# Attention: the products of probabilities and values of two column blocks issued as one run

## Chip, cores and metric

One core of a Trainium2 chip runs the kernel. The metric is the device time of one execution in microseconds; the time of the kernel before is the median of three runs.

## What is computed

One layer of an encoder over 1024 tokens of 1024 channels, float32 throughout: a norm, a wide input projection, four branches (a gated linear recurrence, neighbourhood attention, a state space mixer, pooling), gates, and output products. Only the attention branch is changed. Cut to what matters (8 heads of 64 channels, 16 rows of 64 tokens, 4 column blocks of 16 columns; a block sees 32 columns of 8 rows):

```python
def one_row(r):
    rs = jnp.clip(r - kr // 2, 0, rows - kr)
    k_blk = lax.dynamic_slice_in_dim(kg, rs, kr, axis=1)[:, :, kcol]
    v_blk = lax.dynamic_slice_in_dim(vg, rs, kr, axis=1)[:, :, kcol]
    sc = jnp.einsum('bjqhd,brjkhd->bhjqrk', q_r, k_blk)
    sc = jnp.where(mask, sc + bias[None], -1e30)
    pr = jax.nn.softmax(sc.reshape(sc.shape[:4] + (kr * NA_BAND,)), axis=-1).reshape(sc.shape)
    return jnp.einsum('bhjqrk,brjkhd->bjqhd', pr, v_blk)
```

The changed lines are those of the last einsum, probabilities times values.

## The kernel before

Large products (`mm3`, lines 93 to 95) split each operand into a high and a low part and make three passes of a float32r matmul each. They make up most of the program: the input projection (`z_gen`, `tok_gen`), the merge and the output.

Attention runs in four rounds (`rd`), two heads each. `at_units` goes over two groups of eight rows (`g`) and four column blocks (`j`), so 32 blocks in all, each of 128 queries by 384 keys. A block does the following for its two heads `h`:

- six score matmuls into `ps_s` (line 514), head 0 on partitions 0 to 63 and head 1 on 64 to 127 of the operands;
- bias, maximum, exponential, sum and scaling on DVE and ACT, in the tile `sc` (four buffers);
- three transposes per head into `ps_t` (line 98), copied by ACT into `PT` (line 80; three buffers);
- six products of probabilities and values into `ps_o` (line 536): for each of three key chunks `c`, head 0 (64 columns of the array, output partitions 0 to 63) and then head 1 (output partitions 64 to 127). They are plain float32, and each shows in the trace as two matmuls with a weight load each, so 12 a block and 384 in all. Below, "value products" are these.

The four blocks of a group share one `ps_o` tile, a PSUM bank. When the group is done, ACT copies it into `yb`, and after two groups one DMA writes `yb` out (line 541).

Between two blocks the generator yields, and one piece of other work is emitted: in rounds 0 and 1 the projection for the round two ahead (`at_z`, 24 matmuls of 256 columns a piece, `ps_z`), afterwards pieces of the input projection for other branches (`fill`, 24 matmuls of 512 columns, `ps_z`). So TensorE has two sorts of work in this stage.

The emitted order is not the executed order. The program is built with `schedule_with_timeline_sim=True`: a planner orders the instructions of each engine when the program is built, by dependencies, free buffers and its own estimates of durations. Each engine then executes its queue strictly in that order and waits on semaphores. `add_manual_dep` with the class `NoSync` gives the planner an edge (this one after that one) and adds no semaphore.

The values of a round are in `vb` (one buffer), loaded by 16 DMAs on SP's queue at the start of the round (line 490), with the bias DMAs (line 503) behind them in the same queue. Eleven small loads of constants (`vr`, `gr`, lines 228 to 239) are issued by GpSimd near the start; TensorE transposes them once.

Of the kernel before, what the change touches and what calls it, by code (L numbers as in the profile page):

```python
# [9 lines left out]
F32 = mybir.dt.float32  # L10
# [19 lines left out]
class Kern:  # L30
# [47 lines left out]
    def copy_a(self, out, a, scale=None):  # L78
        if scale is None:
            self.nc.scalar.activation(out, a, AF.Copy)  # L80
        else:
            self.nc.scalar.activation(out, a, AF.Copy, scale=scale)
# [5 lines left out]
    def mm3(self, ps, pairs):  # L88
        """ps = sum over (aH, aL, bH, bL) of a^T b, in three passes each."""
        n = len(pairs)  # L90
        mm = self.nc.tensor.matmul
        for k, (aH, aL, bH, bL) in enumerate(pairs):
            mm(ps, aH, bH, start=(k == 0), stop=False)  # L93
            mm(ps, aH, bL, start=False, stop=False)  # L94
            mm(ps, aL, bH, start=False, stop=(k == n - 1))  # L95
# [4 lines left out]
    def cmul(self, pool, outr, outi, ar, ai, br, bi, shape, neg_im=False):  # L100
        """(outr, outi) = a * b, elementwise complex."""
        t = pool.tile(shape, F32, tag="cm_t", name="cm_t")
        self.mul(outr, ar, br)
        self.mul(t, ai, bi)
        self.sub(outr, outr, t)
        u = pool.tile(shape, F32, tag="cm_u", name="cm_u")
        self.mul(outi, ar, bi)
        self.mul(u, ai, br)
        self.add(outi, outi, u)

    def rsqrt(self, pool, x, n, tag):
        """x [P, n] -> 1/sqrt(x), to float32 accuracy."""
        P = x.shape[0]
        g = pool.tile([P, n], F32, tag=tag + "_g", name=tag + "_g")
        h = pool.tile([P, n], F32, tag=tag + "_h", name=tag + "_h")
        self.ts(h.bitcast(I32), x.bitcast(I32), 1, None, ALU.arith_shift_right)
        self.ts(g.bitcast(I32), h.bitcast(I32), -1, 0x5F3759DF, ALU.mult, ALU.add)
        for _ in range(3):
            self.mul(h, g, g)
            self.stt(h, h, -0.5, x, ALU.mult, ALU.mult)  # L120
            self.stt(g, h, 1.5, g, ALU.add, ALU.mult)
        return g

    def dexp(self, pool, out, x, n):
        """out = exp(x), x [128, n], to float32 accuracy (underflow ends at 1e-38)."""
        t = [pool.tile([128, n], F32, tag=f"de{i}", name=f"de{i}") for i in range(4)]
        xc, nf, r, q = t
        self.ts(xc, x, 88.0, -87.0, ALU.min, ALU.max)
        self.ts(nf, xc, 1.4426950408889634, MAGIC, ALU.mult, ALU.add)
        self.ts(nf, nf, MAGIC, None, ALU.subtract)  # L130
        self.stt(r, nf, -0.693359375, xc, ALU.mult, ALU.add)
        self.stt(r, nf, 2.12194440e-4, r, ALU.mult, ALU.add)
        self.ts(q, r, 1.0 / 5040, None, ALU.mult)
        for c in (1.0 / 720, 1.0 / 120, 1.0 / 24, 1.0 / 6, 0.5, 1.0):
            self.stt(q, q, c, r, ALU.add, ALU.mult)
        self.ts(nf.bitcast(I32), nf, 127.0, 8388608.0, ALU.add, ALU.mult)
        self.stt(out, q, 1.0, nf, ALU.add, ALU.mult)

# [18 lines left out]
    def z_gen(self, parts):  # L157
        """z^T channel tiles. parts: (first column, number of 256-column blocks, consume), with
        consume(ct, half, psum[128 ch, 512 tok]); the weights of a tile are made ready one tile ahead."""
        todo = [(c0 + 256 * b, 2 * b, s, f) for c0, n, f in parts for b in range(n) for s in range(2)]  # L160
        raw = None
        ready = []

        def prep(k):
            nonlocal raw
            c, ct, s, f = todo[k]
            if s == 0:
                raw = self.wload_in(c)
            H, L = self.whl([128, 8, 128])
            self.split(H, L, raw[:, :, s * 128:(s + 1) * 128])  # L170
            ready.append((H, L, ct + s, f))
        prep(0)
        for k in range(len(todo)):
            if k + 1 < len(todo):
                prep(k + 1)
            H, L, ct, f = ready.pop(0)
            for hf in range(2):
                ps = self.ps(self.zt[hf])
                t = slice(hf * 512, hf * 512 + 512)
                self.mm3(ps, [(H[:, k, :], L[:, k, :], self.hnH[k][:, t], self.hnL[k][:, t])  # L180
                              for k in range(8)])
                yield 5.2, 0.55 + (f(ct, hf, ps) or 0.0)
# [5 lines left out]
    def drive(self, main, filler, scale=1.0):  # L188
        """emit main, with pieces of filler wherever the tensor engine would run dry."""
# [10 lines left out]
    def w_tok_halves(self, raw):  # L200
        """a [128, 8, 256] block as rhs: list over k of (H, L) [128, 256]."""
        out = []
        for kh in range(2):
            H, L = self.whl([128, 4, 256])
            self.split(H, L, raw[:, 4 * kh:4 * kh + 4, :])
            out += [(H[:, k, :], L[:, k, :]) for k in range(4)]
        return out

    def tok_gen(self, aH, aL, raw, consume):
        """token-layout product: consume(t, psum[128 tok, 256])."""  # L210
# [40 lines left out]
    def lru_consts(self):  # L251
        """softplus(-lambda) for the LRU, all channel tiles and both directions."""
# [23 lines left out]
    def rel_bias(self):  # L276
        """E[v, q, h, dr, 32]: bias along the band of each kind of column block."""
# [4 lines left out]
        with self.tc.tile_pool(name="nb", bufs=1, reuse_waits="tile") as tmp:  # L282
# [3 lines left out]
            # (v, first q, count, dst column of q0, its step, src column of q0, its step)  # L286
# [157 lines left out]
    def at_z(self, rd, raw=None):  # L444
        """first gives the tiles, then emits the product piece by piece."""
# [12 lines left out]
    def at_prep(self, ap, rd, z):  # L458
# [7 lines left out]
        for sd in range(2):  # L466
# [3 lines left out]
            for hf in range(2):  # L470
                pt = self.ps("t")
                for t in range(4):
                    o = pt[:, t * 128:t * 128 + 128]
                    if sd == 0:   # queries in the order (col block, row, col)
# [8 lines left out]
    def at_units(self, ap, rd, qk, bias, vd):  # L483
# [9 lines left out]
        for g in range(2):  # L493
# [12 lines left out]
            po = self.ps("o")  # L506
            for j in range(4):
# [8 lines left out]
                for h in range(2):  # L516
# [13 lines left out]
                    T = ap.tile([128, 384], F32, tag="PT", name="PT", bufs=3)  # L530
                    self.copy_a(T, pt[:, :384])
                    PT.append(T)
                qc = slice(j * 128, j * 128 + 128)
                for c in range(3):
                    for h in range(2):
                        nc.tensor.matmul(po[hp[h], qc], vb[:, g + c, j, h * 64:h * 64 + 64],  # L536
                                         PT[h][:, c * 128:c * 128 + 128], start=(c == 0), stop=(c == 2))
# [6 lines left out]
    def branch_gate(self, n, c0):  # L544
        """silu of a branch's gate, into DRAM."""
# [164 lines left out]
    def s5_params(self, kp, sp):  # L710
# [29 lines left out]
        # angles into [-pi, pi]; then the cosine's  # L740
# [14 lines left out]
        # powers a^0 .. a^8  # L755
# [10 lines left out]
        # zero-order hold  # L766
# [15 lines left out]
        # Bbar [(d p), g, 32], upper 16 columns zero  # L782
# [10 lines left out]
        # power tables: Q's, slot u: a^u (f), a^(9-u) (b)  # L793
# [8 lines left out]
        # G's, slot t: a^(7-t) (f), a^t (b), times e^{-i 8 theta}  # L802
# [10 lines left out]
        # phasors e^{+-i 8 theta 2^m}  # L813
# [8 lines left out]
        # C^T [(d p), (g c)]  # L822
# [10 lines left out]
        # D on the diagonal of the (quadrant, c) layout of K  # L833
# [13 lines left out]
    def s5_u(self):  # L847
        """c_x, permuted to [ch, t, j] (token 8j + t), into DRAM."""
# [22 lines left out]
    def s5_batch(self, sb, ct):  # L871
# [3 lines left out]
        def bcg(tab, n):   # [128, n, 32] -> [128, 8 g, n, 16]  # L875
            return tab[:, :, g8].rearrange("p n g -> p g n").unsqueeze(3).broadcast_to([128, 8, n, 16])

        def bcc(m, n):     # [128, 8, 16] -> [128, 8 g, n, 16]
# [3 lines left out]
        # u  # L882
# [4 lines left out]
        # G, transposed  # L887
# [22 lines left out]
        # Q = (Re, -Im) of C a^k  # L910
# [11 lines left out]
        # K  # L922
# [29 lines left out]
        # phasors E_j, j < 128  # L952
# [139 lines left out]
    def y_split(self, yp, mp, n, out):  # L1092
        """y_n from DRAM, split; in four pieces."""
# [15 lines left out]
    def branch_products(self, mp, n, Y):  # L1109
        """(m, half, gate, psum) of a branch, gates being whole rows [128, 1024]."""  # L1110
# [163 lines left out]
```

## Time and profile before

| | us |
|---|---|
| median of 3 runs (1428.25 to 1429.24) | 1428.52 |
| span of the profiled execution | 1427.3 |
| around the span (median less span) | 1.2 |
| attention with value products, 160 to 390 us | 230 |

The profile names engines: PE is TensorE's matmuls, PEld its weight loads, DVE the vector, ACT the scalar engine, POOL GpSimd, SP the queue that issues most DMAs. In a timeline, each line is a start, a duration, an engine and a group of instructions that follow each other without a break. Matmuls are pipelined and their ends are modelled, so what a matmul takes of TensorE's time is read from its start to the start of the next, not from its duration.

### The profile page before, as it was taken

The page shows a single profiled execution, that of the slowest core. Times are in us where ns is not written, and L with a number is a line of the kernel's source. Part 1 is how long each engine was busy: PE and PEld are TensorE (multiplying, and loading weights), DVE is VectorE, ACT ScalarE, POOL GpSimd, SP SyncE. Part 2 cuts the span into 40 slices and gives each one's busy share as a digit, 9 for nine tenths or more (in the row PEclk, how much of TensorE's full clock was granted, in tenths as well). Part 3 has the DMA queues.
Part 4 walks back from the last instruction along what each step waited for, and adds up shares of the span by engine and source line. Part 5 has one row for each costly group of instructions (what it writes and reads, how often), then busy time and mean ns, then how long its engine had stood idle before and what let it go on. Part 6 is the DMA issues. An engine that isn't in the chain of part 4 may idle for free.

```text
span 1427.3 us, 20851 instructions
## 1 busy us (share of the span) xinstructions
PE 1413.3 (99%) x8282; PEld 1202.8 (84%) x8282; DVE 838.1 (59%) x1624; ACT 498.8 (35%) x805; POOL 17.4 (1%) x75
## 2 busy tenths in 40 slices
PE   8999999999999999999999999999999999999998
PEld 6999887777788888888888888888888888899998
DVE  6632656334379797979756367446565767532433
ACT  6433555446522222212243544634322222211211
POOL 2100000000000000000000000000000000000000
PEclk9999999999999999999999999999999999999999
DMA  9541223423253242333264143144636654424452
GB/s 314 141 138 46 78 65 81 124 84 104 75 137 91 72 137 89 98 113 107 86 206 151 38 166 107 45 148 151 238 119 251 193 191 162 133 86 149 133 167 88
DMA packets 155139, 182.08 MB, mean 128 GB/s; under 512 B 28944, under 2 KB 129304, under 8 KB 155042
## 3 DMA queue, kind: packets, MB, share of 16 engines
q1 hardware_dynamic: 154690, 180.72, 39.6%
q8 instruction: 65, 1.06, 0.3%
q14 instruction: 32, 0.26, 0.1%
q0 software_dynamic: 352, 0.03, 0.0%
HBM read 127.05 MB, written 54.03 MB: 127 GB/s over the span
## 4 chain that ended last, share of the span: by engine, by line
PE 96%; DVE 2%; ACT 0%; DMA 0%; issue 0%; SPq 0%
PE ps_z L93 20%; PE ps_z L94 19%; PE ps_z L95 19%; PE ps_t L98 4%; PE ps_t L94 3%; PE ps_t L95 3%; PE ps_t L93 3%; PE ps_o L93 3%; PE ps_o L95 3%; PE ps_o L94 3%; PE ps_s L95 3%; PE ps_s L93 3%; PE ps_s L94 3%; PE ps_o L536 2%; PE ps_s L514 2%; PE ps_s L977 1%
## 5 line engine op out<-in xcount | busy, mean ns | idle before, releaser
L93 PE MATMUL ps_z<-hnH,wh 128*128 128x512 f32 x744 | 294.8, 396 | 1.6 <-DVE bgt L58 1.6
L94 PE MATMUL ps_z<-hnL,wh 128*128 128x512 f32 x744 | 293.1, 394 | 0.0
L95 PE MATMUL ps_z<-hnH,wl 128*128 128x512 f32 x744 | 292.8, 394 | 0.0
L64 DVE TENSOR_TENSOR wl<-wr,wh 128x1024 fp32r<-128x1024 f32 x88 | 107.6, 1223 | 131.3 <-ACT wh L80 129.9
L93 PEld LDWEIGHTS ps_z<-hnH,wh 128*128 128x128 f32 x744 | 139.8, 188 | 35.1 <-issue 4.5
L80 ACT ACTIVATE wh<-wr 128x1024 fp32r<-128x1024 f32 x88 | 93.0, 1058 | 208.0 <-PE ps_z L94 97.2
L95 PEld LDWEIGHTS ps_z<-hnH,wl 128*128 128x128 f32 x744 | 139.8, 188 | 30.0 <-issue 1.9
L94 PEld LDWEIGHTS ps_z<-hnL,wh 128*128 128x128 f32 x744 | 139.9, 188 | 28.9 <-issue 1.6
L93 PE MATMUL ps_z<-wh,hnH 128*128 128x256 f32 x384 | 109.0, 286 | 0.4 <-ACT zqk L80 0.4
L95 PE MATMUL ps_z<-wh,hnL 128*128 128x256 f32 x384 | 109.0, 289 | 0.0
L94 PE MATMUL ps_z<-wl,hnH 128*128 128x256 f32 x384 | 108.6, 285 | 0.0
L94 PE MATMUL ps_t<-hnL,wh 128*128 128x512 f32 x216 | 84.3, 390 | 0.0
L95 PE MATMUL ps_t<-hnH,wl 128*128 128x512 f32 x216 | 84.2, 390 | 0.0
L93 PE MATMUL ps_t<-hnH,wh 128*128 128x512 f32 x216 | 84.1, 390 | 0.0
L93 PEld LDWEIGHTS ps_z<-wh,hnH 128*128 128x128 f32 x384 | 73.3, 192 | 2.2 <-issue 1.3
L94 PEld LDWEIGHTS ps_z<-wl,hnH 128*128 128x128 f32 x384 | 73.4, 192 | 1.5 <-issue 1.5
L95 PEld LDWEIGHTS ps_z<-wh,hnL 128*128 128x128 f32 x384 | 72.7, 192 | 1.8 <-issue 1.8
L93 PE MATMUL ps_z<-wh,mH 128*128 128x256 f32 x256 | 73.7, 288 | 0.4 <-DVE fx L61 0.4
L94 PE MATMUL ps_z<-wl,mH 128*128 128x256 f32 x256 | 72.5, 283 | 0.0
L95 PE MATMUL ps_z<-wh,xL 128*128 128x256 f32 x256 | 72.4, 283 | 0.0
L94 PE MATMUL ps_z<-wl,xH 128*128 128x256 f32 x256 | 72.4, 283 | 0.0
L95 PE MATMUL ps_z<-wh,mL 128*128 128x256 f32 x256 | 72.4, 283 | 0.0
(370 smaller groups left out, 2746.4 us busy)
## 6 DMA issues: line engine op xcount, KB each, us to landing
wr<-in_w_in_dram SPq DMA_DIRECT2D x32, 1024.0 KB, 5.3
gd<-gz SPq DMA_DIRECT2D x32, 512.0 KB, 2.9
mgt<-gd SPq DMA_DIRECT2D x32, 512.0 KB, 3.5
sg<-bgt SPq DMA_DIRECT2D x16, 512.0 KB, 3.6
my<-yd SPq DMA_DIRECT2D x16, 512.0 KB, 4.4
mbr<-in_w_branch_dram SPq DMA_DIRECT2D x8, 1024.0 KB, 6.5
bias<-E SPq DMA_DIRECT2D x128, 48.0 KB, 2.0
xt<-in_x_dram SPq DMA_DIRECT2D x8, 512.0 KB, 9.9
```

Source lines behind the costliest of these rows:

```text
L64: self.nc.vector.tensor_tensor(out, a, b, ALU.subtract)
L80: self.nc.scalar.activation(out, a, AF.Copy)
L93: mm(ps, aH, bH, start=(k == 0), stop=False)
L94: mm(ps, aH, bL, start=False, stop=False)
L95: mm(ps, aL, bH, start=False, stop=(k == n - 1))
L98: self.nc.tensor.transpose(ps, src, self.ident[:k, :k])
L514: nc.tensor.matmul(pss[h], q[hp[h], qs], k[(hp[h],) + ks], start=(p == 0), stop=(p == 2))
L536: nc.tensor.matmul(po[hp[h], qc], vb[:, g + c, j, h * 64:h * 64 + 64], PT[h][:, c * 128:c * 128 + 128], start=(c == 0), stop=(c == 2))
L977: nc.tensor.matmul(pv[:, g * 128:g * 128 + 128], Gt[k][:, h * 4 + g, :], U[:, h * 4 + g, :], start=True, stop=True)
```

## The change

`copy_a` returns its instruction. In `at_units`, a block no longer issues its value products; it puts its two `PT` tiles aside. After every second block (`j` 1 and 3) `at_values` issues the products of both blocks, in the same order inside a block, 24 matmuls in all. The first of them gets a `NoSync` edge to the ACT copy that makes the last `PT` tile of the second block. `PT` has six buffers in place of three (1.5 KB per partition each). GpSimd's area for DMA descriptors is set to 1024 bytes by a new argument; it was at its default. Comments and docstrings are removed, which moves line numbers.

```diff
     def copy_a(self, out, a, scale=None):
         if scale is None:
-            self.nc.scalar.activation(out, a, AF.Copy)
-        else:
-            self.nc.scalar.activation(out, a, AF.Copy, scale=scale)
+            return self.nc.scalar.activation(out, a, AF.Copy)
+        return self.nc.scalar.activation(out, a, AF.Copy, scale=scale)
...
             po = self.ps("o")
+            held = []
             for j in range(4):
...
-                    T = ap.tile([128, 384], F32, tag="PT", name="PT", bufs=3)
-                    self.copy_a(T, pt[:, :384])
+                    T = ap.tile([128, 384], F32, tag="PT", name="PT", bufs=6)
+                    last = self.copy_a(T, pt[:, :384])
                     PT.append(T)
-                qc = slice(j * 128, j * 128 + 128)
-                for c in range(3):
-                    for h in range(2):
-                        nc.tensor.matmul(po[hp[h], qc], vb[:, g + c, j, h * 64:h * 64 + 64],
-                                         PT[h][:, c * 128:c * 128 + 128], start=(c == 0), stop=(c == 2))
+                held.append((j, PT))
+                if j % 2:
+                    self.at_values(po, vb, g, held, last)
+                    held = []
                 yield 2.4, 2.0
...
+    def at_values(self, po, vb, g, held, last):
+
+        before = last.ins
+        for j, PT in held:
+            for c in range(3):
+                for h in range(2):
+                    m = self.nc.tensor.matmul(po[64 * h:64 * h + 64, j * 128:j * 128 + 128],
+                                              vb[:, g + c, j, h * 64:h * 64 + 64],
+                                              PT[h][:, c * 128:c * 128 + 128], start=(c == 0), stop=(c == 2))
+                    if before is not None:
+                        self.tc.add_manual_dep(m.ins, before.name, mybir.DependencyInfo(
+                            mybir.DependencyClass.NoSync, mybir.DependencyReason.DATA), reason="one run")
+                    before = None
...
-    nc = _bacc.Bacc("TRN2", target_bir_lowering=False, num_devices=1)
+    nc = _bacc.Bacc("TRN2", target_bir_lowering=False, num_devices=1,
+                     dynamic_dma_scratch_size=1024)
```

## Rows read from the trace of the kernel before

**Rows 1.** The page's first two parts: busy time by engine, TensorE's granted clock.

```profile
span 1427.3 us, 20851 instructions
PE 1413.3 (99%) x8282; PEld 1202.8 (84%) x8282; DVE 838.1 (59%) x1624; ACT 498.8 (35%) x805; POOL 17.4 (1%) x75
...
PEclk9999999999999999999999999999999999999999
```

**Rows 2.** The chain that ended last: shares of the span by engine.

```profile
PE 96%; DVE 2%; ACT 0%; DMA 0%; issue 0%; SPq 0%
```

**Rows 3.** Busy time by stretch: length, PE, PEld, DVE, ACT, POOL, clock, DMA.

```profile
160.00:390.00 230.00, 230.00 (x1434) 171.70 (x1433) 107.69 (x378) 126.17 (x265) 1.25 (x3) 1.00 0.30 89
390.00:1427.30 1037.30, 1030.68 (x5701) 886.60 (x5699) 654.06 (x1059) 302.89 (x407) 4.18 (x50) 1.00 0.41 133
```

**Rows 4.** Groups of instructions, shapes apart: busy us, mean ns, idle before.

```profile
L536 PE MATMUL ps_o<-PT,vb 128*64 128x128 f32 x384 | 39.1, 284 | 0.0
```

**Rows 5.** Timeline of TensorE over one block and a little more: start, duration, group.

```profile
283.50 0.39 PE L93 MATMUL ps_z<-hnH,wh 128*128 128x512 f32 x1
283.72 0.39 PE L94 MATMUL ps_z<-hnL,wh 128*128 128x512 f32 x1
284.04 0.87 PE L536 MATMUL ps_o<-PT,vb 128*64 128x128 f32 x10
284.84 0.55 PE L98 MATMUL ps_t<-ident,sc 128*128 128x128 f32 x3
285.32 0.43 PE L536 MATMUL ps_o<-PT,vb 128*64 128x128 f32 x2
285.68 0.55 PE L98 MATMUL ps_t<-ident,sc 128*128 128x128 f32 x3
...
290.07 0.87 PE L536 MATMUL ps_o<-PT,vb 128*64 128x128 f32 x10
```

**Rows 6.** Timeline of TensorE around a run of twelve, in the last round.

```profile
343.56 0.88 PE L536 MATMUL ps_o<-PT,vb 128*64 128x128 f32 x12
344.37 0.50 PE L95 MATMUL ps_z<-hnH,wl 128*128 128x512 f32 x1
344.70 0.39 PE L93 MATMUL ps_z<-hnH,wh 128*128 128x512 f32 x1
```

**Rows 7.** Timeline of TensorE: transposes between two large products.

```profile
374.26 0.82 PE L98 MATMUL ps_t<-ident,sc 128*128 128x128 f32 x6
374.84 0.48 PE L94 MATMUL ps_z<-hnL,wh 128*128 128x512 f32 x1
375.15 0.40 PE L95 MATMUL ps_z<-hnH,wl 128*128 128x512 f32 x1
```

**Rows 8.** Timeline of TensorE: the scores of one head by themselves.

```profile
305.39 0.44 PE L514 MATMUL ps_s<-qkH 64*128 64x384 f32 x1
...
306.11 0.50 PE L93 MATMUL ps_z<-hnH,wh 128*128 128x512 f32 x1
```

**Rows 9.** Busy time by stretch, score matmuls (L514) alone: length, PE, PEld.

```profile
160.00:390.00 230.00, 33.42 (x174) 18.62 (x174) 1.00 0.30 89
0.00:160.00 160.00, 2.41 (x18) 1.43 (x18) 1.00 0.48 149
```

**Rows 10.** Timeline of ACT: the second head's copy into PT behind rows 5.

```profile
286.33 0.49 ACT L80 ACTIVATE PT<-ps_t 128x384 f32<-128x384 f32 x1 [0.35 <-PE ps_t L98]
```

**Rows 11.** Timeline of ACT near the end of attention.

```profile
379.48 1.06 ACT L80 ACTIVATE wh<-wr 128x1024 fp32r<-128x1024 f32 x1 [1.14 <-PE ps_z L94]
380.55 1.28 ACT L76 ACT_TABLE_LOAD   x1
```

**Rows 12.** Timeline of SP's queue where the first round ends.

```profile
207.31 7.14 SPq L490 DMA_DIRECT2D vb<-vd  x14
```

**Rows 13.** Timeline of POOL: the last of the eleven constant loads.

```profile
30.06 0.48 POOL L239 DMA_DIRECT2D gr<-in_na_k_gain_dram  x1 [0.58 <-DMA vr<-in_lru_b_r_dram]
```

**Rows 14.** Timeline of TensorE: the transposes of these constants.

```profile
58.90 0.41 PE L98 MATMUL ps_t<-ident,vr 13*128 13x13 f32 x4
```

## Prediction

> **What bounds the kernel now.** I read the page's busy times first, then the chain that ended last, then busy time by stretch. The reader is to see three things. TensorE is busy for 1413.3 of 1427.3 us, at the full clock in all forty slices [rows 1], so at 2.4 GHz throughout. The chain that ended last runs for 96% through TensorE [rows 2]. And in the stretch with the value products, 160 to 390 us, TensorE has 230.00 of 230.00 us busy, while DVE has 108 and ACT 126; behind it TensorE lacks 6.6 of 1037.3 us [rows 3]. So in attention nothing hides a microsecond of TensorE's time, and one that is taken away there comes off the end, as the work behind it is bound by TensorE too. But "busy" doesn't say that the time is well used: I went on to the starts of single groups in the timeline, since the spacing of starts is what TensorE really pays.
>
> **What a value product costs now.** Look at one block [rows 5]. Its first value product (two matmuls) stands alone between two groups of transposes: 285.32 to 285.68, 0.36 us. The other five (ten matmuls) come later: 284.04 to 284.84, 0.80 us. In the last round some blocks have all six in one run: twelve matmuls in 343.56 to 344.37, 0.81 us [rows 6]. Ten and twelve cost the same. I take that so: the two heads use different halves of the array's columns and run side by side, so two products, one of each head, take the time of one. Five products are two pairs and one that stands alone, three double steps; six are three pairs, also three. A product standing alone takes two steps. So 0.36 us are two steps and a fixed part, 0.80 us six steps and the fixed part: a step is (0.80 - 0.36) / 4 = 0.11 us, the fixed part 0.36 - 0.22 = 0.14 us.
>
> The neighbours pay as well. Large products follow each other at 0.22 us, but the last one ahead of a value run takes 283.72 to 284.04, 0.32 us: 0.10 more [rows 5]. The first behind one takes 344.37 to 344.70, 0.33: again 0.10 [rows 6]. Three transposes between two value runs take 0.48 us [rows 5], where six between large products take 0.58 and the large product behind them 0.31 [rows 7]: together 0.89 for six steps and a product that would be 6 x 0.11 + 0.23 by themselves. So going over from large products to transposes costs nothing, and the 0.15 us too many in rows 5 belong to the value runs on both sides. A value run therefore costs its neighbours about 0.15 us between transposes, 0.20 between large products, and by half of each 0.17 between one and the other; I take 0.15 for all.
>
> I counted 58 value runs: 26 of two, 26 of ten, 6 of twelve. The group's busy time bears that out: by the durations of such rows, 26 x 0.43 + 26 x 0.87 + 6 x 0.88 = 39.1 us, what the group shows [rows 4], and 52 + 260 + 72 = 384 matmuls.
>
> **What the change removes.** Afterwards there are 16 runs of 24 matmuls, if each stays unbroken. That holds twelve products, six pairs, twelve steps: 0.14 + 12 x 0.11 = 1.46 us.
> - Own time before: 26 x (0.36 + 0.80) + 6 x 0.81 = 35.0 us. After: 16 x 1.46 = 23.4. Saved 11.6. Of it 5.7 are 52 single steps (26 blocks x 2), the rest the fixed parts of 42 runs.
> - Neighbours: 42 runs fewer x 0.15 = 6.3 us saved.
> - Sum 17.9 us.
>
> Here a rule is weighed against the row. The Trainium skill, page "TensorE: Matmul & The Clock Gate", section "Back-to-back issue gap", gives about 56 ns from start to start for 128 columns at the full clock. By that figure the 52 steps would be worth 2.9 us and the sum about 15. The row's 0.11 us per step, at the full clock, is for this kernel's float32 and goes before it.
>
> **Does the run stay unbroken?** The edge binds only the first of the 24 to the last copy. But the products on one `ps_o` already keep their emitted order: head 0's second and third product need only head 0's `PT`, and yet the block's first product runs alone and they come with the second head's [rows 5]. So the other 23 are held with the first, and when it is free all their inputs are there. All 26 runs of ten and 6 of twelve are unbroken now. If each run were cut in two, 16 x (0.14 + 0.15) = 4.6 us would go.
>
> **What it adds or moves, at no cost I can see.** The number of matmuls, weight loads, copies and DMAs is the same; no semaphore is added by the edge. Products wait longer for their turn. Queued behind them on TensorE are transposes, scores and pieces of other products. What the first value product of rows 5's kind waits for is long there: the second head's copy ends at 286.82 [rows 10], the next run of ten starts some 3.2 us later, at 290.07 [rows 5], with large products between. The three additional `PT` buffers let the next blocks' copies go ahead; without them the fourth copy would wait for a held run. At the end of a round `vb` is loaded anew, after its last product: 14 issues take SP 7.14 us [rows 12], and the bias loads stand behind them in SP's queue. The last product of a round comes as late as before, and the first run of the next now needs two blocks, so these loads get slack; large products fill TensorE meanwhile. Without that cover a delay of one run, 1.5 us, at three round ends would cost 4.4.
>
> GpSimd's smaller descriptor area touches eleven small loads. The last is issued at 30.06 us [rows 13], and TensorE uses the constants at 58.90 [rows 14]: 28 us of slack, less the landing.
>
> **The unknown term** is the planner. It orders everything anew, and the scores feel it: the two heads' scores run side by side when they stand next to each other. The three blocks ahead of 160 us show 2.41 / 3 = 0.80 us busy a block [rows 9]; one head alone takes 305.39 to 306.11, 0.72 us to the next start and about 0.80 busy [rows 8], so 1.6 for a split block. 32 blocks at 0.80 are 25.7 us, at 1.6 51.4; the trace has 33.42 + 2.41 = 35.8 [rows 9]. So a new order can gain 10 us or lose 16. Nothing in the change speaks for one side: I take zero, and 6 us either way as the likely part.
>
> **The rivals.**
> - *Scores pair more* (the held products no longer separate them): all or most of the 10 us on top, 1398 to 1405.
> - *Order gets worse*: scores split or runs cut; 6 to 13 us of the 17.9 go, 1417 to 1425.
> - *The change doesn't come through*: the planner fills the space between with other work so that runs are cut and scores split at once, some 17 us back: within 0.2% of before. For it speaks only that the planner doesn't price such runs; against it that no run of ten is cut now.
> - *Slower: TensorE waits for the last copy.* If the planner puts the run right behind the second block's transposes, TensorE stands at the first or a later product for that copy: 0.49 us for it, up to 1.06 + 1.28 more when ACT is at a weight split and a table load [rows 10, 11]: 0.5 to 2.8 us, 16 times, 8 to 45 us. It decides from 17.9 / 16 = 1.1 us a run. At 2.8 the time would be 1428.5 - 17.9 + 45 = 1456. Against it: the 3.2 us between copy and run now, and that other work is always there to put between.
>
> **The numbers.** The sum against the profiled execution: 1427.3 - 17.9 = 1409.4 us of span, and the median stands 1.2 us above the span: 1410.6, so I say 1411. The likeliest case (run unbroken, the rest about as it is) has 60%, with 1405 to 1417; better pairing 12%; worse order 15%; no change 6%; slower 7%. The range 1399 to 1422 leaves out the last two and a part of the others, some 20%. A measurement of this kernel tells about 0.2% (2.9 us) from no change. Faster by over that: 60 + 12 + 15 = 87%; within it 6%; slower 7%.
>
> **What would show it.** The profile after should have 16 groups of 24 value matmuls in the timeline, each about 1.46 us from its start to the next, a group busy of about 16 x 1.53 = 24.5 us (tail included) in place of 39.1; large products and transposes next to each other where runs stood; score matmuls near 36 us busy; no wait of TensorE ahead of value products. I'm wrong if runs are cut, if steps in a run are 0.22 rather than 0.11 (pairs don't carry over from one block to the next), if the scores' busy time grows by over 10 us, or if the stretch shows TensorE idle.

## The result, and the profile after

The kernel after takes 1412.44 us (median of 4 runs, 1412.14 to 1412.93), the one before 1428.47 in the same comparison (1428.25 to 1429.24): a ratio of 0.9885 (95% interval 0.9873 to 0.9898), 16.0 us faster. 1411.0 was forecast, in 1399 to 1422. The profiled span went from 1427.3 [rows 1] to 1410.8 us, 16.5 less.

Line numbers after: value products L548 (L536 before), the three passes of the large products L92 to L94, transposes L97, scores still L514. First the page's busy times of the kernel after, in the columns of [rows 1]:

```profile
span 1410.8 us, 20838 instructions
PE 1397.0 (99%) x8282; PEld 1200.5 (85%) x8282; DVE 838.0 (59%) x1624; ACT 497.1 (35%) x805; POOL 17.6 (1%) x75
```

The same 8282 matmuls take 16.3 us less of TensorE, and it is still busy for 99%. The stretches say where the time came from. In the kernel after, busy time by stretch, cut so that the same work lies on either side as in [rows 3]:

```profile
160.00:373.40 213.40, 213.40 (x1433) 169.41 (x1432) 107.55 (x378) 124.18 (x265) 1.24 (x3) 1.00 0.32 95
373.40:1410.80 1037.40, 1030.86 (x5702) 886.55 (x5700) 654.13 (x1059) 303.06 (x407) 4.19 (x50) 1.00 0.41 133
```

The stretch with the value products shrank from 230.0 to 213.4 us, TensorE being busy throughout as before; all behind it takes 1037.4 where it took 1037.3. So what was taken from TensorE in attention came off the end in full. The groups of instructions after, shapes apart (busy us, mean ns, idle before):

```profile
L97 PE MATMUL ps_t<-ident,sc 128*128 128x128 f32 x192 | 29.4, 278 | 0.0
L548 PE MATMUL ps_o<-PT,vb 128*64 128x128 f32 x384 | 24.9, 277 | 0.0
```

The transposes' group in the kernel before:

```profile
L98 PE MATMUL ps_t<-ident,sc 128*128 128x128 f32 x192 | 33.4, 287 | 0.0
```

The value products' group went from 39.1 [rows 4] to 24.9 us; the transposes, which weren't touched, from 33.4 to 29.4 us, as they often stood beside a value run. The timeline of TensorE after, around a run between large products:

```profile
321.10 0.39 PE L94 MATMUL ps_z<-hnH,wl 128*128 128x512 f32 x1
321.32 0.39 PE L92 MATMUL ps_z<-hnH,wh 128*128 128x512 f32 x1
321.64 1.53 PE L548 MATMUL ps_o<-PT,vb 128*64 128x128 f32 x24
323.10 0.50 PE L93 MATMUL ps_z<-hnL,wh 128*128 128x512 f32 x1
323.44 0.40 PE L94 MATMUL ps_z<-hnH,wl 128*128 128x512 f32 x1
323.68 0.40 PE L92 MATMUL ps_z<-hnH,wh 128*128 128x512 f32 x1
```

The run takes 321.64 to 323.10, 1.46 us, as forecast, and its neighbours still pay: 0.32 and 0.34 us to the next start where a large product otherwise takes 0.22 to 0.24 (the first line and the last but one). Fifteen of the sixteen runs look like this. The first doesn't; the timeline of TensorE after, at its place:

```profile
169.77 1.09 PE L548 MATMUL ps_o<-PT,vb 128*64 128x128 f32 x14
170.79 0.44 PE L514 MATMUL ps_s<-qkH 64*128 64x384 f32 x1
171.07 0.34 PE L514 MATMUL ps_s<-qkL,qkH 64*128 64x384 f32 x1
171.34 0.87 PE L548 MATMUL ps_o<-PT,vb 128*64 128x128 f32 x10
172.14 0.87 PE L97 MATMUL ps_t<-ident,sc 128*128 128x128 f32 x6
```

Fourteen matmuls are seven products; the eighth is the first that reads the last `PT` tile. So there are 17 runs, not 16.

I added up the timelines of both kernels from the start of each group to the start of the next, which leaves out modelled tails; below, a group's "own time" is this sum. Value products 35.07 to 23.74 us (-11.3), transposes of `sc` -4.6, large products -1.5, scores 32.32 to 33.53 (+1.2): together -16.3. The scores' busy time by stretch, scores (L514) alone, after and over the whole span:

```profile
0.00:1410.00 1410.00, 37.03 (x192) 21.06 (x192) 1.00 0.40 129
```

That is 1.2 us above 33.42 + 2.41 [rows 9]. Of 96 pairs of score matmuls (the same pass, one of each head) 59 stand in one unbroken run of scores, 66 did before.

### The profile page after: what moved, and what is told of

Same layout as the page of the kernel before. It is cut to its first block, busy times and chain, and to the rows that moved or that the text cites. A ratio compares the mean times of both kernels' runs of the same rounds, so it can differ in the third digit from the quotient of the medians.

```text
span 1410.8 us, 20838 instructions
## 1 busy us (share of the span) xinstructions
PE 1397.0 (99%) x8282; PEld 1200.5 (85%) x8282; DVE 838.0 (59%) x1624; ACT 497.1 (35%) x805; POOL 17.6 (1%) x75
## 4 chain that ended last, share of the span: by engine, by line
PE 96%; DVE 2%; ACT 0%; DMA 0%; issue 0%; SPq 0%
PE ps_z L92 20%; PE ps_z L93 20%; PE ps_z L94 20%; PE ps_t L97 4%; PE ps_t L93 3%; PE ps_t L94 3%; PE ps_t L92 3%; PE ps_o L92 3%; PE ps_o L93 3%; PE ps_o L94 3%; PE ps_s L92 3%; PE ps_s L93 3%; PE ps_s L94 3%; PE ps_s L514 2%; PE ps_o L548 2%; PE ps_s L990 1%
## 5 line engine op out<-in xcount | busy, mean ns | idle before, releaser
L92 PE MATMUL ps_z<-hnH,wh 128*128 128x512 f32 x744 | 294.4, 396 | 1.6 <-DVE bgt L58 1.6
L94 PE MATMUL ps_z<-hnH,wl 128*128 128x512 f32 x744 | 292.3, 393 | 0.0
L92 PEld LDWEIGHTS ps_z<-hnH,wh 128*128 128x128 f32 x744 | 139.8, 188 | 35.4 <-issue 4.6
L94 PEld LDWEIGHTS ps_z<-hnH,wl 128*128 128x128 f32 x744 | 139.8, 188 | 29.3 <-issue 0.9
L92 PE MATMUL ps_z<-wh,hnH 128*128 128x256 f32 x384 | 109.2, 287 | 0.4 <-ACT zqk L80 0.4
L94 PE MATMUL ps_z<-wh,hnL 128*128 128x256 f32 x384 | 108.5, 287 | 0.0
L94 PE MATMUL ps_t<-hnH,wl 128*128 128x512 f32 x216 | 84.1, 389 | 0.0
L92 PE MATMUL ps_t<-hnH,wh 128*128 128x512 f32 x216 | 84.1, 389 | 0.0
L92 PEld LDWEIGHTS ps_z<-wh,hnH 128*128 128x128 f32 x384 | 73.2, 191 | 3.0 <-issue 2.1
L92 PE MATMUL ps_z<-wh,mH 128*128 128x256 f32 x256 | 73.6, 288 | 0.4 <-DVE fx L61 0.4
L94 PEld LDWEIGHTS ps_z<-wh,hnL 128*128 128x128 f32 x384 | 72.7, 191 | 1.0 <-issue 1.0
L94 PE MATMUL ps_z<-wh,xL 128*128 128x256 f32 x256 | 72.3, 283 | 0.0
L94 PE MATMUL ps_z<-wh,mL 128*128 128x256 f32 x256 | 72.3, 283 | 0.0
```

## The experiments

The first five tell the cause apart; the next three part the change into its pieces; the last three follow what the change left lying.

**The roomier buffers alone.** The kernel before with the two other edits of the change:

```diff
-                    T = ap.tile([128, 384], F32, tag="PT", name="PT", bufs=3)
+                    T = ap.tile([128, 384], F32, tag="PT", name="PT", bufs=6)
...
+                     dynamic_dma_scratch_size=1024)
```

> The kernel before with six PT buffers and the descriptor area of 1024 bytes, and nothing else. Theory (array shape): the runs of value products stay 26 of two, 26 of ten, 6 of twelve, so 1428.5 within 1 us. Rival (roomier buffers): about 1412.

Measured: 1428.65 us, ratio 0.9999 (0.9990 to 1.0009). The value products' group is what it was:

```profile
L536 PE MATMUL ps_o<-PT,vb 128*64 128x128 f32 x384 | 39.1, 284 | 0.0
```

The rival that the room brings the gain falls; the room and GpSimd's area, tried together, cost and gain nothing here.

**Fewer runs without holding anything back.** The kernel before, with those buffers, emits the later head's product first, so that a block's products can only start once both `PT` tiles are there:

```diff
...
                 for c in range(3):
-                    for h in range(2):
+                    for h in (1, 0):
                         nc.tensor.matmul(po[hp[h], qc], vb[:, g + c, j, h * 64:h * 64 + 64],
...
```

> Nothing is held back: a block's six value products stand where they stood before, but head 1's come ahead of head 0's, so that the first already needs the block's last copy; the program then has 32 runs of twelve matmuls. PT has six buffers and the descriptor area is 1024 bytes, as in the change. Theory (array shape: a run costs 0.14 us itself and 0.15 at its neighbours, a step 0.11 when the heads alternate): own 32 x 0.81 = 25.9 in place of 35.1 us, neighbours 26 runs fewer x 0.15 = 3.9 less, so 13.1 us less than before, 1415.3 (1411 to 1418 with what the scores do). Rival (the gain is from the roomier buffers and the order that they allow): about 1412, the same as the change.

Measured: 1410.79 us, 0.9876 (0.9861 to 0.9891), just below the range. The group:

```profile
L536 PE MATMUL ps_o<-PT,vb 128*64 128x128 f32 x384 | 28.0, 281 | 0.0
```

One of its 32 runs of twelve in the timeline of TensorE:

```profile
283.32 0.88 PE L536 MATMUL ps_o<-PT,vb 128*64 128x128 f32 x12
284.12 0.87 PE L98 MATMUL ps_t<-ident,sc 128*128 128x128 f32 x6
```

Each run takes 0.80 us (283.32 to 284.12); the value products' own time is 25.81, where 32 x 0.81 = 25.9 was counted on. Most of the 4.5 us by which it beat the sum are scores: in this order 78 of 96 pairs stand side by side, and their own time falls by 3.6 us against before. The time by itself lies nearer to the rival's 1412 than to the 1415.3 of the theory; that the buffers alone give nothing (above), and the 32 runs at the price forecast, are what tells the two apart. So swapping two loop values, with no edge, is worth as much as the whole change (its median is 1.7 us lower, the intervals of the ratios overlap): the runs are worth less, and the scores make up for it. The swap with three buffers wasn't tried.

**Shape or number type.** Does a run cost its fixed part because it uses half of the array's columns, or because it is plain float32 between float32r products? The kernel after, with both heads' values as the weight, 128 columns wide, one `ps_o` per head, of which ACT copies the half that is wanted:

```diff
...
-                    m = self.nc.tensor.matmul(po[64 * h:64 * h + 64, j * 128:j * 128 + 128],
-                                              vb[:, g + c, j, h * 64:h * 64 + 64],
+                    m = self.nc.tensor.matmul(po[h][:, j * 128:j * 128 + 128],
+                                              vb[:, g + c, j, :],
...
```

> The kernel after, but each value product takes both heads' values as 128 weight columns, so that it runs in the whole array and not in half of its columns; each head has its own PSUM tile of which the unused half is not read. Twice the multiplications, the same number of matmuls. Theory (array shape): no fixed part and nothing at the neighbours, but no two products share a step: 384 x 0.11 = 42 us in place of 23.7 + 3, 16 us slower than after, 1428. Rival (what costs is the change between the two number types, float32r and float32, not the shape): the runs keep their 0.29 us each on top, 25 runs, 1435.

Measured: 1427.88 us, 0.9994 (0.9984 to 1.0003). The timeline of TensorE in this kernel:

```profile
332.87 0.39 PE L94 MATMUL ps_z<-hnH,wl 128*128 128x512 f32 x1
333.10 2.84 PE L550 MATMUL ps_o<-PT,vb 128*128 128x128 f32 x24
335.77 0.82 PE L97 MATMUL ps_t<-ident,sc 128*128 128x128 f32 x6
336.34 0.48 PE L92 MATMUL ps_z<-hnH,wh 128*128 128x512 f32 x1
```

The run takes 2.67 us for 24 steps, 0.111 each, with no fixed part; the large product ahead of it takes its usual 0.23 us, the transposes behind it 0.57, as between large products [rows 7]. The 25 runs into which this kernel's order cuts the value products have 42.53 us of own time, 384 steps of 0.111. The products are still plain float32 between float32r products. So the price sits at the change between half and full width, not at the number type, and the heads side by side are what halves the time. That each head also has a `ps_o` of its own here wasn't tried apart. The Trainium skill, page "TensorEngine Tiling (Array Packing)", section "Key Properties", says that changing the tiling mode, as against only the tile, drains the engine; the trace agrees that such a change costs time (0.14 us in the run and 0.15 at its neighbours, none of either here), though not by what.

**Do the heads have to alternate?** The kernel after, with all three products of a head together:

```diff
-            for c in range(3):
-                for h in range(2):
+            for h in range(2):
+                for c in range(3):
```

> The kernel after, but inside a block head 0's three products come first and then head 1's three, so the heads no longer alternate; 16 runs of 24 stay. Theory (array shape, steps shared by the two heads): the steps go from 12 to some 24 a run, 0.14 + 24 x 0.11 = 2.78 in place of 1.46 us, 16 x 1.32 = 21 us slower than after, 1433. Rival (only the number of runs counts, the order of the heads doesn't): 1412.

Measured: 1416.53 us, 0.9916 (0.9899 to 0.9933), which neither had. The timeline of TensorE around one run:

```profile
323.98 0.39 PE L92 MATMUL ps_z<-hnH,wh 128*128 128x512 f32 x1
324.30 1.80 PE L548 MATMUL ps_o<-PT,vb 128*64 128x128 f32 x24
326.03 0.50 PE L93 MATMUL ps_z<-hnL,wh 128*128 128x512 f32 x1
```

1.73 us from start to start: not 2.78 as if heads in turn took a step for each matmul, and 0.27 (2.5 steps) more than alternating. So matmuls of the two halves overlap though they don't stand next to each other. The single starts in the trace, which a timeline merges, show how. In the kernel after, the 24 matmuls of a run start in twos, 6 to 7 ns apart, one two every 0.109 us (the first after 0.160). With the heads in turn there are two rows of twelve starts, each again 0.160 and then 0.109 us apart, and in all 16 runs the second row sets in 0.275 us behind the first: the whole of the difference. What fits all runs seen: 0.14 us and 0.11 for each matmul of the half that has more of them, plus the delay with which the other half gets its first work. Ten matmuls behind one product are four and six: 0.14 + 0.66 = 0.80 [rows 5]. Fourteen, in the broken run above, are eight and six: 0.14 + 0.88 = 1.02, and 169.77 to 170.79 is 1.02.

**What the edge holds.** The kernel after with an issue, and so an edge, for each block:

```diff
-                if j % 2:
+                if True:
```

> The kernel after, but a block's products are issued behind the block itself, the first with the edge to the block's last copy; six buffers. By the program's order the edge doesn't make one run of twelve: 25 runs of two and 25 of ten stay, as the edge only lets the first product be placed when the copy has been placed, and the second needs the copy's result. Theory (array shape): own 25 x 1.16 + 1.46 + 5 x 0.81 = 34.5, 0.6 less than before, two runs fewer; 1427, or some 3 less by the scores (23 blocks whole, 19 before): 1423 to 1428. Rival (the edge itself helps): 1412 to 1416.

Measured: 1429.03 us, 1.0004 (0.9995 to 1.0014), a little above the range. The timeline of TensorE over one block:

```profile
284.02 0.43 PE L548 MATMUL ps_o<-PT,vb 128*64 128x128 f32 x2
284.38 0.50 PE L93 MATMUL ps_z<-hnL,wh 128*128 128x512 f32 x1
284.72 0.40 PE L94 MATMUL ps_z<-hnH,wl 128*128 128x512 f32 x1
285.05 0.87 PE L548 MATMUL ps_o<-PT,vb 128*64 128x128 f32 x10
```

The first product, with its edge, goes off by itself as before, and the one that reads the last `PT` comes with the rest: 25 of the 32 blocks are still cut after the first product, and of the value products' own time only 0.5 us is saved. Up to the last value product this kernel is 4.2 us ahead of the one before, by transposes and scores in the main; 4.3 us are lost behind it (last section). So the edge holds a product until the last copy has its place in the order, not until it is done. With two blocks seven products that need nothing of the last copy stand ahead of the eighth, and the run holds in 15 of 16; that they fill the time of the copy in the planner's reckoning is my reading and wasn't tried by itself.

**Two blocks without the edge.**

```diff
-        before = last.ins
+        before = None
```

> The kernel after without the edge: two blocks' value products are emitted together behind the second block, and the planner may place the first as soon as its own PT is copied. By the program's order, 19 runs of two, 16 of ten, 15 of twelve and one of six matmuls then. Theory (array shape): own 19 x 0.36 + 16 x 0.80 + 15 x 0.81 + 0.5 = 32.3 us, 2.8 less than before, and 7 runs fewer at 0.15: 1425 (1421 to 1428 with the scores). Rival (emitting them together is what helps, the edge adds little): 1412 to 1416.

Measured: 1427.45 us (1425.36 to 1428.63), 0.9992 (0.9982 to 1.0002). 51 runs: 19 of two, 16 of ten, 15 of twelve, one of six. The planner takes each block's products when they are ready, whatever the order in which they were emitted. The value products' own time falls by 2.7 us as worked out, the transposes by 1.7, and 4.0 us are lost behind the last value product (below, the last section). Emitting two blocks together saves 2.7 us of the value products' own time, the edge with one block 0.5; both together save 11.3.

**Four buffers.**

```diff
-                    T = ap.tile([128, 384], F32, tag="PT", name="PT", bufs=6)
+                    T = ap.tile([128, 384], F32, tag="PT", name="PT", bufs=4)
```

> The kernel after with four PT buffers, just enough for a held run, in place of six. Theory (array shape; TensorE has other work to put between): the runs stay (15 of 24, one of 14, one of 10 by the program's order), so 1412.4 within 3. Rival (the room in PT carries the gain, as the next blocks' copies otherwise wait for the run): 1418 or more, with TensorE waiting ahead of transposes.

Measured: 1410.59 us, 0.9874 (0.9857 to 0.9890), the value products' group 24.9 us as with six. Four hold two blocks, and the fifth and sixth bring nothing. With four the time is even 1.9 us lower than with six; 1.1 us of that is the scores' own time (32.39 in place of 33.53), so most of it is again the order.

**Four blocks in one run.**

```diff
-                if j % 2:
+                if j == 3:
...
-                    T = ap.tile([128, 384], F32, tag="PT", name="PT", bufs=6)
+                    T = ap.tile([128, 384], F32, tag="PT", name="PT", bufs=10)
```

> The kernel after, with the products of all four blocks of a group held back and ten PT buffers: 8 runs of 48 matmuls. Theory (array shape): own 8 x (0.14 + 24 x 0.11) = 22.2 in place of 23.7 us, neighbours 9 runs fewer x 0.15 = 1.4: 2.9 us less than after, 1409.6 (1407 to 1413 with the scores). Rival (a run of 2.8 us holds up the next blocks' scores and transposes, which TensorE then waits for): 1412 or more, with waits of TensorE ahead of transposes.

Measured: 1409.81 us, 0.9866 (0.9848 to 0.9883). The group:

```profile
L548 PE MATMUL ps_o<-PT,vb 128*64 128x128 f32 x384 | 22.7, 275 | 0.0
```

Eight runs of 48; the median is 2.6 us lower than after. By the timelines the value products' own time falls from 23.74 to 22.17 us, and transposes and large products take 1.2 less: 2.7 us for nine runs, 0.30 each, near the 0.14 + 0.15 of the prediction. Its time can't be told from that of the kernel with four buffers (1410.59).

**The scores held together.** The term that the prediction left at zero, taken on its own. The kernel after, with an edge that puts a block's first score matmul behind the previous block's maximum having been negated, so that head 0's scores can't run off ahead of head 1's:

```diff
+        self.read = None
...
-                        nc.tensor.matmul(pss[h], q[hp[h], qs], k[(hp[h],) + ks], start=(p == 0), stop=(p == 2))
+                        m = nc.tensor.matmul(pss[h], q[hp[h], qs], k[(hp[h],) + ks], start=(p == 0), stop=(p == 2))
+                        if p == 0 and h == 0 and self.read is not None:
+                            self.tc.add_manual_dep(m.ins, self.read.name, mybir.DependencyInfo(
+                                mybir.DependencyClass.NoSync, mybir.DependencyReason.DATA), reason="pair")
...
-                    self.ts(nm, mx, -1.0, None, ALU.mult)
+                    r = nc.vector.tensor_scalar(nm, mx, -1.0, None, ALU.mult)
+                    self.read = r.ins
```

> The kernel after, with one more edge without a semaphore: a block's first score matmul comes behind the DVE instruction that negates the maximum of head 1 of the block before, so that both heads' PSUM tiles are free when the scores start. By the program's order, 29 of 32 blocks then have their six score matmuls in one run, 17 in the kernel after. Theory (array shape holds for scores too: two heads in different halves of the rows run side by side, and each run costs its neighbours about 0.2): own from 33.5 to some 25 us, 15 runs fewer x 0.2 = 3: 1401 (1398 to 1405). Rival (the edge delays the softmax chain and TensorE waits): 1412 or more.

Measured: 1400.40 us, 0.9802 (0.9786 to 0.9817). 94 of 96 pairs stand side by side. Busy time by stretch of the scores alone (now L515):

```profile
0.00:1398.00 1398.00, 26.84 (x192) 15.49 (x192) 1.00 0.40 130
```

One block's scores in the timeline of TensorE:

```profile
288.86 0.45 PE L515 MATMUL ps_s<-qkH 64*128 64x384 f32 x2
289.14 0.34 PE L515 MATMUL ps_s<-qkL,qkH 64*128 64x384 f32 x2
289.32 0.34 PE L515 MATMUL ps_s<-qkH,qkL 64*128 64x384 f32 x2
289.59 0.50 PE L94 MATMUL ps_z<-hnL,wh 128*128 128x512 f32 x1
```

Both heads take 288.86 to 289.59, 0.73 us, where one head alone took 0.72 [rows 8]: the second head is free. The busy time falls from 37.03 to 26.84, near the 25.7 that the prediction worked out as the floor, and the run from 1412.4 to 1400.4. By the timelines the scores' own time falls by 9.1 us, and transposes and large products take 2.5 less, with 35 score runs in place of 50.

**Four blocks and the scores held together**, the last two edits in one kernel.

> The two last kernels in one: 8 runs of 48 value matmuls, ten PT buffers, scores with the edge (31 of 32 blocks whole by the program's order). Theory: both gains add up, 2.9 + 11 us: 1398 (1395 to 1402). Rival (the waits of either): 1405 or more.

Measured: 1397.82 us (1397.56 to 1398.33), 0.9785 (0.9769 to 0.9800). It beats both kernels, by 30.4 us the one before in its own comparison (1428.27) and by 14.6 the one after. The value products' group:

```profile
L553 PE MATMUL ps_o<-PT,vb 128*64 128x128 f32 x384 | 22.7, 275 | 0.0
```

Busy time by stretch of the scores alone:

```profile
0.00:1396.00 1396.00, 26.15 (x192) 15.41 (x192) 1.00 0.40 130
```

**The scores held together in the kernel before**: the score edge shown above, put into the kernel before by itself.

> The kernel before with the edge for the scores alone. By the program's order 25 blocks have their six score matmuls in one run (19 before), and the value products stand in 20 runs of two, 21 of ten, 10 of twelve, one of fourteen. Theory (array shape): value products own 20 x 0.36 + 21 x 0.80 + 10 x 0.81 + 0.9 = 33.0, 2 less, 6 runs fewer 0.9; scores own some 5 less, 12 runs fewer x 0.2 = 2.4: 1418 (1414 to 1422). Rival (pairing the scores only helps together with held products): 1428.

Measured: 1419.54 us, 0.9937 (0.9922 to 0.9952). Scores' own time -6.4 us, transposes -3.2, value products -1.9 (their busy time 36.8 us), and 4.5 us lost behind the last value product (last section). The two edits touch different time: the value runs are worth 16 us, the scores 9 (with that loss) to 12.

## Why the prediction was right

*TensorE bounds the stretch, and what it is given comes off the end.* Right: 16.6 us less in the stretch, nothing given back behind it.

*The price of a run.* Right in size: 1.46 us for 24 matmuls, measured 1.46; 11.6 us of own time forecast, 11.3 measured. The difference is the seventeenth run, 0.29 us. A step is 0.11 us in every run seen. The figure of the Trainium skill that was set against the row (some 56 ns for 128 columns, page "TensorE: Matmul & The Clock Gate", section "Back-to-back issue gap") is there the gap of an isolated matmul; for a stream of weight loads and matmuls the section gives some 81 ns, which the prediction left out. Neither is the 0.11 us that this kernel's float32 shows.

*The neighbours.* Right: 0.15 us for each run that goes, now 41 of them, 6.2 us; the transposes (-4.6) and large products (-1.5) lost 6.1. The full-width kernel, in which no value run changes the width, bears it out: against it these two take 8.4 us more before, for 58 runs, and 2.2 more after, for 17, so 0.14 and 0.13 a run.

*Side by side only as neighbours.* Right in what it gave, wrong in its reason. The prediction took two products to share a step because they stand next to each other; with the heads in turn they still overlap for all but 0.275 us of a run. For the order of this change both readings give the same number.

*The run stays unbroken.* The step that failed in part. That a first product which is free has all its inputs was inferred from products of one block going together; but the edge ties it only to the place of the last copy, and one run of 16 was cut there. It cost 0.3 us; with one block to an edge 25 of 32 blocks are cut. That the other fifteen held is more than the prediction's reason could promise: the number came out, but in this step it was in part luck.

*Buffers and GpSimd's area at no cost.* Right, and the buffers beyond four at no gain.

*The planner's order.* The term left at zero was +1.2 us of scores, inside its six either way, and most of the 1.6 us by which the sum of 17.9 exceeded the 16.3 measured (the rest is 0.3 of own time and 0.2 at the neighbours; the tenth too many is rounding). That 10 us were to be had there was right as well: holding the scores together took 12 us off the kernel after, 9.1 of them the scores' own. But the change didn't bring them, so this rival fell, and that of a worse order came only as far as these 1.2.

*The slower case.* It didn't come: the list of TensorE's waits after has no value product in it, and no wait that the one before hadn't. Even runs of 48 brought none.

What stays open is why one order splits 37 pairs of scores (after), another 30 (before) and a third 18 (heads swapped); that is the planner's, and only its effect was measured.

## What to carry to other kernels

Where an engine is busy for the whole of a stretch, look at the starts of its groups: short runs of another shape among large ones may cost more at their edges than in their work, here 0.29 us a run. Two halves of the array give their second half for nothing only if both have work at the time, so keep such partners near each other, and look for every pair of that kind in the stage (scores as well as values) before you rearrange one. An ordering edge to a producer holds until that has its place in the order; tie it so that whatever reads the last result stands late in the run, or emit the latest input's reader first.

## What the runs showed of the hardware that was not expected

**The two halves of the array work ahead of each other** by more than one product: 24 matmuls in 1.73 us with the heads in turn, in two rows of starts that lie 0.275 us apart. How far ahead they can get, the runs don't tell.

**A new order costs somewhere else, in part by the clock.** In three kernels (no edge, an edge for each block, the kernel before with its scores held together) what lies behind the last value product took 4.0, 4.3 and 4.5 us longer than in the kernel before. The place is the state space stage, some 100 us behind attention and not edited, which the planner ordered anew. The list of TensorE's waits (total, times, longest) in the kernel with an edge for each block, and then in the kernel after:

```profile
PE ps_z L92 <- DVE bgt L58: 3.7, 2, 2.0
```

```profile
PE ps_z L92 <- DVE bgt L58: 1.6, 3, 0.8
```

The planned order lets TensorE wait 2.0 us for DVE in one place where the longest such wait was 0.8. What follows, in the timeline of TensorE of the kernel with an edge for each block:

```profile
498.64 0.50 PE L92 MATMUL ps_z<-hnH,wh 128*128 128x512 f32 x1 [1.96 <-DVE bgt L58]
498.98 0.40 PE L93 MATMUL ps_z<-hnL,wh 128*128 128x512 f32 x1
499.22 0.42 PE L94 MATMUL ps_z<-hnH,wl 128*128 128x512 f32 x1
499.46 0.62 PE L92 MATMUL ps_z<-hnH,wh 128*128 128x512 f32 x1
499.87 0.63 PE L93 MATMUL ps_z<-hnL,wh 128*128 128x512 f32 x1
500.29 0.63 PE L94 MATMUL ps_z<-hnH,wl 128*128 128x512 f32 x1
```

From 499.46 us, less than a microsecond behind the wait, the large products stand 0.41 to 0.42 us apart instead of 0.23. Busy time by stretch of the kernel before with its scores held together, at the same place in the work (clock in the third column from the right):

```profile
486.40:489.80 3.40, 1.45 (x8) 1.08 (x7) 3.40 (x5) 0.60 (x1) 0.00 (x0) 1.00 0.43 142
489.80:493.20 3.40, 3.40 (x10) 2.63 (x9) 3.40 (x5) 0.00 (x0) 0.00 (x0) 0.50 0.92 323
```

The granted clock goes from 1.00 to 0.50, from 2.4 to 1.2 GHz, for 3.4 us, behind a stretch in which TensorE was busy for 1.45 of 3.40 us; all three kernels show it, and no other kernel's trace does in this stage. That the wait alone brings the fall isn't shown: the kernel with an edge for each block has a second wait of this sort, 1.7 us long, at 648.4 us, and behind it the clock stays at 1.00; in the kernel without the edge two waits of 0.6 and 1.5 us stood ahead of the fall. In the kernel with an edge for each block, the waits are 2.1 us more and eight large products some 0.2 us longer, 1.6: 3.7 of its 4.3 us. So the two cases that missed their sums upwards (an edge for each block, and in part the two blocks without the edge) did so far away from the edit, and a small gain in one stage can be eaten by a wait that a new order makes in another.
